# All 31 convolution taps of channel tile 7 on TensorE for both token chunks, as two token phases by 64 channels; and chunk A's first two output tiles side by side

## The chip, the cores and the metric

The kernel runs on one core of a Trainium2 chip. The metric is the device time of one execution in microseconds (us). The engines are named as the profile names them: PE is TensorE (PEld its weight load), DVE is VectorE, ACT is ScalarE, POOL is GpSimd, and SP is the queue that issues most of the loads. Line numbers such as L128 are those of the kernel before; two of its helper lines record nearly everything, L128 every instruction of DVE, ACT and POOL, and L151 every matmul, so groups are told apart by the names of their tiles.

## The reference

A decoder trunk of two layers on 1024 tokens of 1024 channels. The first layer mixes tokens with a causal Conformer convolution, the second with a multi-scale pooling mixer; each is followed by a SwiGLU feed-forward of width 2816. The change touches only the convolution:

```python
def conformer_conv(h, w1, b1, w_dw, b_dw, ln_g, ln_b, w2, b2):
    u = h @ w1 + b1
    a, g = jnp.split(u, 2, axis=-1)
    u = a * jax.nn.sigmoid(g)
    u = lax.conv_general_dilated(          # depthwise, causal, CONV_WIDTH = 31 taps
        u, w_dw[:, None, :], window_strides=(1,), padding=[(CONV_WIDTH - 1, 0)], ...) + b_dw
    u = jax.nn.silu(layer_norm(u, ln_g, ln_b))     # over the 1024 channels
    return u @ w2 + b2

def reference(...):
    for i in range(DEPTH):                 # DEPTH = 2
        ...                                # adaLN: shift, scale and gate columns from c
        h = modulate(rms_norm(x, norm_mix_g[i]), sh_m, sc_m)
        y = conformer_conv(h, ...) if i % 2 == 0 else multiscale_pool(h, ...)
        x = x + (1.0 + g_m)[:, None, :] * y
        h = modulate(rms_norm(x, norm_ffn_g[i]), sh_f, sc_f)
        x = x + (1.0 + g_f)[:, None, :] * swiglu_ffn(h, ...)
    return rms_norm(x, final_g)
```

## The kernel before

**Layout.** Channels lie on the 128 partitions, tokens on the free axis. The 1024 channels are 8 tiles (0 to 7), the 1024 tokens two chunks of 512: A (the first) and B. Matmuls run in a 32-bit format that rounds its operands, so each value is split into a high and a low part, and `products()` issues three matmuls for each product: high by high, high by low, low by high. A weight of 128x1024 arrives in a `raw` buffer (ring of three), ScalarE casts it to its high part (`w<-raw`), VectorE subtracts to get the low one (`w<-raw,w`), and the pair stays in a ring of five (`W_BUFS`) until its products are over. Some loads are issued on GpSimd's queue, most on SP's.

**The convolution module.** For each tile, `conv_in` multiplies h by w1 into two PSUM banks, `a` and `g`, 24 matmuls each. `conv_glu` takes ScalarE's sigmoid of g into `t`, and VectorE multiplies (`u<-a,vecs,t`). Then the 31 taps follow. Most are done by `Taps` tasks: on VectorE an accumulation in one of two extra PSUM banks (`ca<-u,vecs,ca`, one instruction for each tap; the first is `ca<-u,vecs` alone), or on ScalarE a product `pr` that GpSimd adds to a partial sum `pa`; at the end VectorE adds `pa` to `ca` and applies the last tap (`u<-u,vecs,ca`). Two tiles have taps on TensorE, by matmuls with diagonal matrices (`tap<-us,w`, us being the split u): 15 of tile 6's for chunk A, and all 31 of tile 7's for chunk A (`PE_TAPS = {6: 15, 7: CW}`, `pe_taps`). The diagonals come as six weights of eight blocks (`wdg`). Chunk B's tiles 6 and 7 are done by `Taps` like the others. The last 30 tokens of chunk A's u are kept in `uhalo` for chunk B.

**The layer norm** (`layer_norm_silu`) adds the eight convolved tiles on VectorE (`acc`; the seventh sum ends it), multiplies by a matrix of ones on PE (`mean<-acc,ones`), centres, squares, sums, takes the root (`var`, `rstd` on PE), and applies SiLU into the split pairs `v`. `conv_out` then multiplies by w2, one bank `y` for each output tile, and updates x.

**The order.** PE runs in the order in which the program is written, and that is the order of a list of units: chunk A's w1 tiles, the last of chunk A together with the same tiles of chunk B, most of chunk B's w1 tiles, the TensorE taps, the rest of chunk B's w1 tiles, w2 of chunk A, chunk B's last w1 tile, and the first feed-forward's head for chunk A (products `p` by w_gate and w_up, `dn` by w_down), in the course of which chunk B's taps and layer norm go on beside it; then w2 of chunk B. Between products, `pace()` lets the tasks of the other engines take steps as long as the planner's estimated clocks of these engines lie less than 4 us ahead of PE's. A task that needs PE yields a name of the table `DELAY`, and its next PE instruction is written that many estimated us later. VectorE, ScalarE, GpSimd and SP run their own queues in order, and an instruction waits only for its data and for a free buffer. The six ordinary PSUM banks serve all of `a`, `g`, `tap`, `mean`, `y` in turn.

The adaLN columns that the feed-forward needs first are handled amid the taps: `columns_done` sends sums `t` through PE (`adac<-quarters,t`), and VectorE adds a bias (`mod<-adac,vecs`).

Of the kernel before, what the change touches and what calls it, by code (L numbers as in the profile page):

```python
# [53 lines left out]
DIAGS = 8  # L54
LOAD = {"load": 4.0, "both": 9.5, "slow": 6.0, "next": 4.0, "dots": 4.0}
# [16 lines left out]
DELAY = {"stats": 2.75, "spread": 3.0, "soon": 0.5, "settled": 3.0, "later": 5.0, "root": 3.4}  # L72
# [4 lines left out]
for _name, _w in (  # L77
    ("ada_b", DEPTH * 6 * KT), ("norm_mix_g", DEPTH * KT), ("norm_ffn_g", DEPTH * KT),
    ("conv_b1", 2 * KT), ("conv_bdw", KT), ("conv_ln_g", KT), ("conv_ln_b", KT), ("conv_b2", KT),
    ("c", KT), ("pool_ls", KT), ("final_g", KT), ("conv_wdw", CW * KT),  # L80
):
    _COLS[_name] = _n
    _n += _w
# [18 lines left out]
def tap_groups(p):  # L102

    n = PE_TAPS[p]

    todo = list(range(CW - 1, -1, -1) if n == CW else range(CW - 3, CW - 3 - 2 * n, -2))
# [27 lines left out]
def trunk(ctx, tc, xT, c, vec, ada, adan, w1f, w1, wdg, w2, wgu, wdn, wds, wpl, out):  # L134
# [597 lines left out]
    def conv_u(ch, p):  # L732
        u = st["u", ch.i, p] = wslot(ch, "u", p)
        if ch.i == 0:
# [5 lines left out]
    def conv_glu(ch, p, ba, bg, own=False):  # L740
# [50 lines left out]

    def split_u(p):
# [6 lines left out]
    def pe_taps(p):  # L799
# [4 lines left out]
        for i, js in enumerate(groups):  # L804
            def emit(take, i=i, js=js):
# [3 lines left out]
                for q, j in enumerate(js):  # L809
                    full = PE_TAPS[p] == CW  # L810
                    o = (CW - 1 - j) // 2 * 2 if full else CW - 3 - j
                    c = j + o if full else 0
                    products(b[:, o:], wt, q, [v[:, c : c + A.n - o] for v in st["us", p]], j == groups[0][0], j == groups[-1][-1])
                    if q % 4 == 3:
                        pace()
                if i == len(groups) - 1:
                    if full:
                        S_.activation(st["u", 0, p][:, HALO:], b, AF.Identity, bias=V("conv_bdw", p))
                        st["taps", 0][p] = True
                    else:  # L820
                        T["taps", 0, p].other = b
# [86 lines left out]
    def layer_norm_silu(ch):  # L908
# [17 lines left out]
        yield "soon" if ch.i else "stats"  # L926
# [1330 lines left out]
```

## Time and profile before

| what | value |
|---|---|
| median of three runs | 1677.97 us (1677.6, 1677.97, 1678.09) |
| the profiled execution, its time | 1675.66 us |
| its span in the trace | 1673.9 us |
| PE busy | 1651.8 us, 7550 matmuls |
| DVE busy | 1310.0 us, 1867 instructions |
| ACT busy | 804.1 us, 1090 instructions |
| POOL busy | 487.4 us, 567 instructions |
| w1, taps and layer norm of chunk A | up to about 300 us |
| first feed-forward's head, with chunk B's taps and layer norm beside it | about 300 to 460 us |

Of the views below, the page gives busy time by engine and the chain of work that ended last. A row of the windows begins with the window's bounds in us and its length; then come the busy us and the instructions in brackets for PE, PEld, DVE, ACT and POOL; then the granted clock of PE, the DMA engines' share and the GB/s moved. A row of the waits reads: engine, tile and line, what released it, the total us, the count, the longest. A row of the timeline reads: start, length, engine, line, operation, out<-in, shape, and behind an x how many instructions of that kind are put together; in square brackets the wait before it and what ended it. A row of groups ends with the busy us and the mean ns of one, and behind the last bar the idle time before them and what ended most of it.

Convolution's place in the time: the adaLN columns of PE come at 181 us, the last TensorE tap at about 200 us, chunk A's mean at 205 us, chunk B's at 417 us.

### The profile page before, as it was taken

The numbers are of one execution on the slowest core, as the hardware profiler recorded it, in microseconds if no ns is written. First come the engines' busy times: TensorE is split into PE (matmuls) and PEld (weight loads), VectorE is DVE, ScalarE is ACT, GpSimd is POOL, SyncE is SP. The second block draws the span as 40 slices with busy tenths as digits, with TensorE's granted clock in tenths as the row PEclk, the third lists the DMA queues.
The fourth block names the chain that finished last, engine by engine and source line by source line (L and its number), as shares of the span: only waits on it lengthen the run. The fifth ranks groups of instructions, "written<-read, shape, count | busy, mean of one in ns | idle before, by whom it ended". The sixth has DMA issues, their size and how long they took to land.

```text
span 1673.9 us, 21194 instructions
## 1 busy us (share of the span) xinstructions
PE 1651.8 (99%) x7550; PEld 1351.2 (81%) x7550; DVE 1310.0 (78%) x1867; ACT 804.1 (48%) x1090; POOL 487.4 (29%) x567
## 2 busy tenths in 40 slices
PE   7999999999999999999999999999999999999997
PEld 5777878787888888888888888888888888888887
DVE  8889899799759888888678957848777766658657
ACT  3669696867546332332234436637322222244354
POOL 3587777796002111221100502101111111000013
PEclk9999999999999999999999999999999999999999
DMA  8958997828776888886965959866777776686664
GB/s 301 295 176 228 225 236 205 226 78 241 229 234 168 278 264 287 282 272 206 400 231 164 285 155 283 247 211 199 189 225 222 220 227 183 207 273 207 192 170 126
DMA packets 117180, 378.60 MB, mean 226 GB/s; under 512 B 12369, under 2 KB 14545, under 8 KB 117074
## 3 DMA queue, kind: packets, MB, share of 16 engines
q1 hardware_dynamic: 79664, 245.63, 41.6%
q0 software_dynamic: 36832, 131.09, 32.5%
q8 instruction: 59, 0.97, 0.2%
q10 hardware_dynamic: 578, 0.53, 0.1%
q14 instruction: 47, 0.39, 0.1%
HBM read 310.61 MB, written 62.39 MB: 223 GB/s over the span
## 4 chain that ended last, share of the span: by engine, by line
PE 88%; POOL 3%; DVE 2%; DMA 2%; issue 2%; ACT 2%; DVEq 0%; SPq 0%; POOLq 0%; ACTq 0%
PE a L151 24%; PE dn L151 23%; PE e L151 14%; PE p L151 10%; PE y L151 6%; POOL pa L128 3%; PE first L151 3%; PE g L151 2%; PE tap L151 2%; DMA adaw<-in_adan_dram 1%; DMA s<-in_wds_dram 1%; PE ada L151 1%; ACT w L128 1%; DMA w<-in_wgu_dram 1%; PE var L151 1%
## 5 line engine op out<-in xcount | busy, mean ns | idle before, releaser
L128 ACT CAST w<-raw 128x1024 fp32r<-128x1024 f32 (+1 forms) x247 | 254.6, 1033 | 305.5 <-PE dn L151 56.9
L128 DVE TENSOR_TENSOR w<-raw,w 128x1024 fp32r<-128x1024 f32 (+1 forms) x173 | 209.3, 1214 | 62.2 <-ACT w L128 61.9
L151 PE MATMUL a<-n,w 128*128 128x512 f32 x1056 | 246.8, 389 | 0.2
L151 PE MATMUL p<-h,w 128*128 128x512 f32 x1056 | 243.7, 390 | 1.2 <-DMA w<-in_wgu_dram 1.0
L128 POOL TENSOR_TENSOR pa<-pa,pr 128x512 f32<-128x512 f32 x159 | 225.3, 1500 | 29.0 <-ACT pr L128 23.7
L151 PEld LDWEIGHTS p<-h,w 128*128 128x128 f32 x1056 | 197.3, 188 | 43.7 <-DMA w<-in_wgu_dram 1.4
L151 PEld LDWEIGHTS a<-n,w 128*128 128x128 f32 x1056 | 198.0, 188 | 42.2 <-DVE r L128 1.1
L151 PE MATMUL dn<-hi,w 128*128 128x512 f32 (+1 forms) x768 | 226.2, 377 | 0.4 <-DVE w L128 0.4
L151 PE MATMUL dn<-g,w 128*128 128x512 f32 x864 | 199.1, 390 | 0.2 <-DVE x L128 0.2
L151 PEld LDWEIGHTS dn<-g,w 128*128 128x128 f32 x864 | 161.7, 188 | 34.7 <-DVE x L128 0.6
L128 DVE SCALAR_TENSOR_TENSOR ca<-u,vecs,ca 128x512 f32<-128x512 f32 x246 | 170.6, 747 | 0.5
L151 PEld LDWEIGHTS dn<-hi,w 128*128 128x128 f32 x768 | 141.2, 188 | 27.0 <-DVE w L128 0.9
L151 PE MATMUL dn<-lo,w 128*128 128x512 f32 (+1 forms) x384 | 144.3, 376 | 0.0
L151 PE MATMUL a<-t,w 128*128 128x512 f32 x528 | 123.3, 389 | 0.0
L151 PE MATMUL e<-t,w 128*128 128x512 f32 x528 | 123.3, 389 | 0.0
L151 PE MATMUL e<-b,w 128*128 128x512 f32 x528 | 123.3, 389 | 0.0
L128 ACT ACTIVATE pr<-u,vecs 128x512 f32<-128x512 f32 x159 | 108.4, 717 | 25.0 <-POOL pa L128 19.7
L151 PEld LDWEIGHTS a<-t,w 128*128 128x128 f32 x528 | 99.1, 188 | 20.7
L151 PEld LDWEIGHTS e<-t,w 128*128 128x128 f32 x528 | 99.1, 188 | 20.6
L151 PEld LDWEIGHTS e<-b,w 128*128 128x128 f32 x528 | 99.1, 188 | 20.6
L1191 POOL DMA_DIRECT2D raw<-in_wgu_dram x41 | 36.5, 889 | 271.5 <-DVE r L128 104.2
L128 ACT CAST hi<-op 128x1024 fp32r<-128x1024 f32 (+1 forms) x52 | 48.5, 935 | 87.1 <-PE dn L151 77.2
(191 smaller groups left out, 2449.4 us busy)
## 6 DMA issues: line engine op xcount, KB each, us to landing
raw<-in_wgu_dram SPq DMA_DIRECT2D x132, 512.0 KB, 4.7
raw<-in_wds_dram SPq DMA_DIRECT2D x48, 512.0 KB, 6.0
adaw<-in_ada_dram POOLq DMA_DIRECT2D x48, 512.0 KB, 6.8
kinds<-k POOLq DMA_DIRECT2D x42, 512.0 KB, 7.7
raw<-in_wgu_dram POOLq DMA_DIRECT2D x41, 512.0 KB, 7.3
raw<-in_w_dram SPq DMA_DIRECT2D x36, 512.0 KB, 6.6
op<-kinds SPq DMA_DIRECT2D x36, 512.0 KB, 4.8
adaw<-in_adan_dram SPq DMA_DIRECT2D x32, 512.0 KB, 5.5
```

Source lines behind the costliest of these rows:

```text
L128: self.last = self.order(getattr(self.eng, name)(out, *args, **kw))
L151: last_mm[0] = nc.tensor.matmul(out, lhsT, rhs, start=start, stop=stop, skip_group_check=more).ins.name
L1191: d = order(nc.gpsimd.dma_start(w[i], wgu[l, fp, src], accum_op=ADD))
```

## The change

Tile 7 leaves the `Taps` tasks altogether. Its u is no longer kept as 128 channels by 512 tokens: `halves` stacks the even tokens of 64 channels on partitions 0 to 63 and the odd tokens of the same 64 channels on partitions 64 to 127, once for each half g of the channels, for both chunks in one buffer (15 zero columns in front, then 256 token pairs of A, then 256 of B). A matrix of 128x128 then holds up to four taps (from either phase to either phase) for each of 64 channels, and 16 such blocks with shifts of whole pairs cover the 31 taps. One product is 512 columns wide and serves both chunks at once: 2 groups of 16 blocks of 3 matmuls, 96, in place of 31 times 3, 93, of 512 down to 482 columns for chunk A alone. The number of weights stays at six. Each group's bank is written back to u's ordinary layout by four ScalarE instructions of 64x256.

With it the mean of chunk A gets a delay of its own in the planner's table (4.6 in place of 2.75), and `conv_out` of chunk A puts its first two output tiles side by side as that of chunk B did.

By instructions, PE has 3 matmuls more; DVE has 17 `ca<-u,vecs,ca` fewer, eight instructions of 64x256 more, and some single ones fewer, 13 fewer in sum; ACT has 4 fewer in sum (11 `pr` fewer); POOL has 14 fewer in sum (11 `pa` fewer).

```diff
@@ constants, and one row of the table of planning delays
+HALF = P // 2          # 64 channels
+NM = (CW + 1) // 2     # 16 blocks
+LEAD = NM - 1          # 15 token pairs of history
-DELAY = {"stats": 2.75, "spread": 3.0, ...
+DELAY = {"mean": 4.6, "stats": 2.75, "spread": 3.0, ...

@@ conv_u: tile 7's u needs no halo in front
         u = st["u", ch.i, p] = wslot(ch, "u", p)
+        if PE_TAPS.get(p) == CW:
+            return u

@@ conv_glu: tile 7
-        if ch.i == 0 and PE_TAPS.get(p) == CW:
-            V_.scalar_tensor_tensor(ba, ba, V("conv_b1", p), sg, op0=ADD, op1=MUL)
-            pair = wpair(B, "us", F32R)
-            hi, lo = st["us", p] = [pair[:, i, : ch.width] for i in range(2)]
-            for part in (hi, lo):
-                G_.memset(part[:, HALO - 2 : HALO].bitcast(F32), 0.0)
-            S_.copy(hi[:, HALO:], ba)
-            V_.tensor_tensor(lo[:, HALO:], ba, hi[:, HALO:].bitcast(F32), op=SUB)
-            S_.copy(uhalo[:, p, :], ba[:, ch.n - HALO :])
+        if PE_TAPS.get(p) == CW:
+            halves(ch, p, ba, sg)
             return

@@ new: u by token phase (f) and channel half (g)
+    def halves(ch, p, ba, sg):
+        n = ch.n // 2
+        t = temp(ch.n).rearrange("p (g n) -> p g n", g=2)
+        for g in range(2):
+            at = slice(HALF * g, HALF * g + HALF)
+            for f in range(2):
+                V_.scalar_tensor_tensor(t[HALF * f : HALF * f + HALF, g], ba[at].rearrange("p (n f) -> p f n", f=2)[:, f], V("conv_b1", p)[at],
+                                        sg[at].rearrange("p (n f) -> p f n", f=2)[:, f], op0=ADD, op1=MUL)
+        if ch.i == 0:
+            st["us", p] = [wpair(B, "us", F32R) for _ in range(2)]
+            for part in st["us", p]:
+                G_.memset(part[:, :, :LEAD].bitcast(F32), 0.0)
+        hi, lo = (part[:, :, LEAD + ch.i * n : LEAD + ch.i * n + n] for part in st["us", p])
+        S_.copy(hi, t)
+        V_.tensor_tensor(lo, t, hi.bitcast(F32), op=SUB)

@@ new: the taps of tile 7, both chunks in one product of 512 columns
+    def pe_halves(p):
+        blocks = [(g, m) for g in range(2) for m in range(NM)]
...
+                    if m == 0:
+                        st["tap", p] = bank("tap")
+                    b = st["tap", p]
+                    products(b, wt, q, [part[:, g, m : m + 512] for part in st["us", p]], m == 0, m == NM - 1)
+                    if q % 4 == 3:
+                        pace()
+                    if m == NM - 1:
+                        for ch in chunks:
+                            n = ch.n // 2
+                            d = st["u", ch.i, p][HALF * g : HALF * g + HALF, HALO:].rearrange("p (n f) -> p f n", f=2)
+                            for f in range(2):
+                                at = slice(HALF * f, HALF * f + HALF)
+                                S_.activation(d[:, f], b[at, n * ch.i : n * ch.i + n], AF.Identity, bias=V("bdw_halves", g)[at])
+                            if g:
+                                st["taps", ch.i][p] = True
...

@@ pe_taps: the case of all 31 taps
                 for q, j in enumerate(js):
-                    full = PE_TAPS[p] == CW
-                    o = (CW - 1 - j) // 2 * 2 if full else CW - 3 - j
-                    c = j + o if full else 0
-                    products(b[:, o:], wt, q, [v[:, c : c + A.n - o] for v in st["us", p]], j == groups[0][0], j == groups[-1][-1])
+                    o = CW - 3 - j
+                    products(b[:, o:], wt, q, [v[:, : A.n - o] for v in st["us", p]], j == groups[0][0], j == groups[-1][-1])
...
-                    if full:
-                        S_.activation(st["u", 0, p][:, HALO:], b, AF.Identity, bias=V("conv_bdw", p))
-                        st["taps", 0][p] = True
-                    else:
-                        T["taps", 0, p].other = b
+                    T["taps", 0, p].other = b

@@ layer_norm_silu: the planner's delay between acc and the mean
-        yield "soon" if ch.i else "stats"
+        yield "soon" if ch.i else "mean"

@@ conv_out: the output tiles that share a unit
-        for ds in [(0, 1) if ch.i else (0,), *(() if ch.i else ((1,),)), *((d,) for d in range(2, KT))]:
+        for ds in [(0, 1), *((d,) for d in range(2, KT))]:

@@ trunk
     for p in PE_TAPS:
-        for u in pe_taps(p):
+        for u in pe_halves(p) if PE_TAPS[p] == CW else pe_taps(p):
             unit(*u)
...
-    taps(B, *some, *rest[: len(rest) - HOLD - HOLD_LN])
+    taps(B, *[p for p in some if PE_TAPS.get(p, 0) < CW], *rest[: len(rest) - HOLD - HOLD_LN])

@@ host: the weights of the blocks (dense 128 x 128 in place of diagonals)
+    dense = np.zeros((len(whole), 2, NM, 2, HALF, 2, HALF), np.float32)
+    for i, p in enumerate(whole):
+        for m in range(NM):
+            for f in range(2):
+                for o in range(2):
+                    j = 2 * (m - LEAD) + CW - 1 + f - o
+                    if 0 <= j < CW:
+                        dense[i, :, m, f, range(HALF), o, range(HALF)] = taps[j, p].reshape(2, HALF).T
+    dense = dense.reshape(-1, DIAGS, P, P).transpose(0, 2, 1, 3)
```

Since the planner writes the order, three places show what it makes of the change. First VectorE, from the adaLN columns on (`mod`), ahead of chunk A's mean; ca_1559 and ca_1591 before, ca_1566 and ca_1622 after, are the tap banks of chunk A's last two `Taps` tiles, acc_1453 and acc_1459 the sum of the tiles. Before:

```order
L128 TENSOR_TENSOR mod<-adac_1792,vecs 128x8
L128 SCALAR_TENSOR_TENSOR ca_1559<-u_721,vecs,ca_1559 128x512
L128 SCALAR_TENSOR_TENSOR ca_1591<-u_721,vecs,ca_1591 128x512
L128 SCALAR_TENSOR_TENSOR ca_1559<-u_721,vecs,ca_1559 128x512
L128 SCALAR_TENSOR_TENSOR ca_1591<-u_721,vecs,ca_1591 128x512 x3
L128 TENSOR_TENSOR ca_1559<-pa_1529,ca_1559 128x512
L128 SCALAR_TENSOR_TENSOR ca_1591<-u_721,vecs,ca_1591 128x512
L128 SCALAR_TENSOR_TENSOR u_721<-u_721,vecs,ca_1559 128x512
L128 SCALAR_TENSOR_TENSOR ca_1591<-u_721,vecs,ca_1591 128x512
L128 TENSOR_TENSOR acc_1453<-acc_1453,u_721 128x512
```

And now, the start and (from the end of the first tile on) the corresponding rows:

```order
L130 TENSOR_TENSOR mod<-adac_1796,vecs 128x8
L130 SCALAR_TENSOR_TENSOR ca_1622<-u_721,vecs,ca_1622 128x512
L130 SCALAR_TENSOR_TENSOR ca_1566<-u_721,vecs,ca_1566 128x512
...
L130 SCALAR_TENSOR_TENSOR ca_1622<-u_721,vecs,ca_1622 128x512
L130 TENSOR_TENSOR ca_1566<-pa_1556,ca_1566 128x512
L130 SCALAR_TENSOR_TENSOR ca_1622<-u_721,vecs,ca_1622 128x512
L130 SCALAR_TENSOR_TENSOR u_721<-u_721,vecs,ca_1566 128x512
L130 SCALAR_TENSOR_TENSOR ca_1622<-u_721,vecs,ca_1622 128x512
L130 TENSOR_TENSOR acc_1459<-acc_1459,u_721 128x512
```

Between `mod` and the partial sum's addition (`ca<-pa,ca`) stood 6 taps and now stand 17; from `mod` to the last sum of acc, in all, there were 33 instructions, 21 of them such taps, and there are 41, 29 of them taps.

Second PE, at the end of the TensorE taps, where chunk A's mean stands. Before:

```order
L151 MATMUL tap_1779<-us_1229,w_1735 128x484 x6
L151 MATMUL tap_1779<-us_1229,w_1735 128x482 x3
L151 MATMUL a_1975<-h_801,w_1769 128x512 x3
...
L151 MATMUL a_1975<-h_808,w_1769 128x512 x3
L151 MATMUL mean_2010<-acc_1962,ones 128x512
L151 MATMUL g_1976<-h_801,w_1829 128x512 x3
```

And now:

```order
L153 MATMUL tap_1889<-us_1233,w_1742 128x512
L153 MATMUL tap_1889<-us_1232,w_1742 128x512
L153 MATMUL a_1996<-h_801,w_1776 128x512 x3
...
L153 MATMUL a_1996<-h_808,w_1776 128x512 x3
L153 MATMUL mean_2031<-acc_1983,ones 128x512
L153 MATMUL g_1997<-h_801,w_1834 128x512 x3
```

The mean stands at the same place, behind the 24 matmuls of the next w1 tile's `a`; what moved is its operand's chain on VectorE.

Third PE in the feed-forward's head, where chunk B's mean stands. Before:

```order
L151 MATMUL p_3852<-h_2808,w_3749 128x512 x3
L151 MATMUL dn_3974<-g_3744,w_3796 128x512 x3
L151 MATMUL dn_3975<-g_3744,w_3796 128x512 x3
L151 MATMUL dn_3976<-g_3744,w_3796 128x512 x3
L151 MATMUL dn_3977<-g_3744,w_3796 128x512 x3
L151 MATMUL mean_3990<-acc_3961,ones 128x512
L151 MATMUL dn_3974<-g_3843,w_3848 128x512 x3
```

And now:

```order
L153 MATMUL p_3763<-h_2838,w_3592 128x512 x3
L153 MATMUL p_3763<-h_2839,w_3592 128x512 x3
L153 MATMUL p_3763<-h_2840,w_3592 128x512 x3
L153 MATMUL mean_3791<-acc_3748,ones 128x512
L153 MATMUL p_3667<-h_2841,w_3609 128x512 x3
```

It moved 108 matmuls ahead, out of the `dn` products into the `p` products before them; the `var` and `rstd` products behind it follow in their turn.

More of the change, by code (lines that the diff above doesn't have):

```diff
@@ L71 @@
 LATER = 300
-DELAY = {"stats": 2.75, "spread": 3.0, "soon": 0.5, "settled": 3.0, "later": 5.0, "root": 3.4}
+DELAY = {"mean": 4.6, "stats": 2.75, "spread": 3.0, "soon": 0.5, "settled": 3.0, "later": 5.0, "root": 3.4}
 DELAY_BEHIND = {"stats": 8, "spread": 4, "soon": 0.5, "settled": 3.0, "later": 8}
@@ L79 @@
     ("conv_b1", 2 * KT), ("conv_bdw", KT), ("conv_ln_g", KT), ("conv_ln_b", KT), ("conv_b2", KT),
-    ("c", KT), ("pool_ls", KT), ("final_g", KT), ("conv_wdw", CW * KT),
+    ("c", KT), ("pool_ls", KT), ("final_g", KT), ("conv_wdw", CW * KT), ("bdw_halves", 2),
 ):
@@ L104, in tap_groups @@
     n = PE_TAPS[p]
-    todo = list(range(CW - 1, -1, -1) if n == CW else range(CW - 3, CW - 3 - 2 * n, -2))
+    todo = list(range(CW - 3, CW - 3 - 2 * n, -2))
     return [todo[i : i + DIAGS] for i in range(0, len(todo), DIAGS)]
@@ L790, in conv_in, with emit_of, emit @@
         unit(emit, *[w1[p, i] for p in tiles for i in range(2)])
+    def halves(ch, p, ba, sg):
[15 more added lines that the diff above has]
+        blocks = [(g, m) for g in range(2) for m in range(NM)]
+        first = sum(len(tap_groups(q)) for q in PE_TAPS if q < p)
+        def emit_of(these):
+            def emit(take):
+                wt = take()
+                for q, (g, m) in enumerate(these):
+                    if m == 0:
[13 more added lines that the diff above has]
+                                st["taps", ch.i][p] = True
+            return emit
+        return [(emit_of(blocks[i : i + DIAGS]), wdg[first + i // DIAGS]) for i in range(0, len(blocks), DIAGS)]
     def split_u(p):
@@ L2207 @@
         ada_b, norm_mix_g, norm_ffn_g, conv_b1, conv_bdw, conv_ln_g, conv_ln_b, conv_b2, c, pool_ls, final_g, conv_wdw)])
+    whole = [p for p in PE_TAPS if PE_TAPS[p] == CW]
+    vec = np.concatenate([vec, np.tile(np.asarray(conv_bdw).reshape(KT, 2, HALF)[whole].reshape(-1, HALF), (1, 2))])
     def tiles(w, f):
@@ L2219 @@
     taps = np.asarray(conv_wdw)[0].reshape(CW, KT, P)
-    groups = [(p, js) for p in sorted(PE_TAPS) for js in tap_groups(p)]
+    groups = [(p, js) for p in sorted(PE_TAPS) if PE_TAPS[p] < CW for js in tap_groups(p)]
     diag = np.zeros((len(groups), P, DIAGS, P), np.float32)
@@ L2224 @@
             diag[i, range(P), q, range(P)] = taps[j, p]
+    dense = np.zeros((len(whole), 2, NM, 2, HALF, 2, HALF), np.float32)
[7 more added lines that the diff above has]
+    dense = dense.reshape(-1, DIAGS, P, P).transpose(0, 2, 1, 3)
+    diag = np.concatenate([diag, dense])
     down = np.asarray(ffn_w_down).reshape(DEPTH, NP, 2, P, 2, D // 2)
@@ L2238 @@
         "w1": A(np.stack([t1[:KT], t1[KT:]], axis=1)),
-        "wdg": A(diag.reshape(len(groups), P, -1)),
+        "wdg": A(diag.reshape(len(diag), P, -1)),
         "w2": A(tiles(np.asarray(conv_w2)[0], KT)),
```

## The prediction

> **What bounds the kernel now.** I read the page first, then the windows, then PE's waits, then the timelines around each place that the change touches. The page:
>
> ```profile
> span 1673.9 us, 21194 instructions
> PE 1651.8 (99%) x7550; PEld 1351.2 (81%) x7550; DVE 1310.0 (78%) x1867; ACT 804.1 (48%) x1090; POOL 487.4 (29%) x567
> PE 88%; POOL 3%; DVE 2%; DMA 2%; issue 2%; ACT 2%; DVEq 0%; SPq 0%; POOLq 0%; ACTq 0%
> ```
>
> TensorE is busy for 99% of the span and carries 88% of the chain. A window in the feed-forward shows its pace, and PE's waits between 60 and 460 us, where all of the changed work lies, are these four:
>
> ```profile
> 700.00:800.00 100.00, 100.00 (x443) 82.81 (x442) 81.20 (x111) 28.85 (x34) 19.48 (x34) 1.00 0.79 249
> ...
> PE p L151 <- DMA w<-in_wgu_dram: 1.0, 1, 1.0
> PE ada L151 <- DMA adaw<-in_adan_dram: 0.3, 1, 0.3
> PE dn L151 <- DVE x L128: 0.2, 1, 0.2
> PE p L151 <- ACT r L128: 0.2, 1, 0.2
> ```
>
> 443 products in 100 us are 0.226 us each. All four waits together are 1.7 us. So work that leaves VectorE, ScalarE and GpSimd here cannot make the kernel faster by more than 1.7 us: PE does not wait for it. What can cost is work added to PE, or a product that now stands ahead of its operand.
>
> **The change part by part.** *PE's own work.* Tile 7 took 31 taps of three products for chunk A, 512 down to 482 columns wide. It now takes 32 blocks of three products, all 512 wide, for both chunks. By the order, 12 products stand ahead of the adaLN columns (adac) in both kernels; then 81 stood before chunk A's next w1 product, and now 84.
>
> ```profile
> 181.16 0.51 PE L151 MATMUL adac<-quarters,t 128*128 128x4 f32 x4
> 181.52 18.61 PE L151 MATMUL tap<-us,w 128*128 128x508 f32 x81
> ...
> 199.97 5.62 PE L151 MATMUL a<-h,w 128*128 128x512 f32 x24
> 205.43 1.02 PE L151 MATMUL mean<-acc,ones 128*128 128x512 f32 x2
> ```
>
> The 81 took 199.97 - 181.52 = 18.45 us. The 24 behind them took 205.43 - 199.97 = 5.46 us, 0.2275 each, and 84 such take 19.11 us: +0.66 us, all of it on PE's path. The first group of 12 changes by less than 0.05 us.
>
> *Chunk A's mean.* This is where I expect the loss. The order puts the mean product behind 24 products of the next w1 tile, as before, so PE is there at 205.43 + 0.66 = 206.09 us. Its operand acc is the sum of the eight convolved tiles, made on VectorE. That chain before:
>
> ```profile
> 169.38 0.67 ACT L128 ACTIVATE t<-g,vecs 128x512 f32<-128x512 f32 x1
> ...
> 170.08 0.75 DVE L128 SCALAR_TENSOR_TENSOR u<-a,vecs,t 128x512 f32<-128x512 f32 x1
> 170.75 9.30 DVE L128 SCALAR_TENSOR_TENSOR ca<-u,vecs,ca 128x512 f32<-128x512 f32 x14
> 181.70 0.17 DVE L128 TENSOR_TENSOR mod<-adac,vecs 128x8 f32<-128x8 f32 x1 [1.65 <-PE adac L151]
> 181.78 4.30 DVE L128 SCALAR_TENSOR_TENSOR ca<-u,vecs,ca 128x512 f32<-128x512 f32 x6
> ...
> 203.35 1.50 DVE L128 TENSOR_TENSOR acc<-acc,u 128x512 f32<-128x512 f32 x2
> ```
>
> VectorE runs in order and waits 1.65 us for adac, which PE reaches at 181.16 us. So everything behind the mod instruction starts at 181.78 us, however early VectorE was. From there to acc it was busy all but about 0.5 us:
>
> ```profile
> L128 DVE SCALAR_TENSOR_TENSOR ca<-u,vecs,ca 128x512 f32<-128x512 f32 x21 | 14.8, 750 | 0.1
> L128 DVE TENSOR_TENSOR ca<-pa,ca 128x512 f32<-128x512 f32 x3 | 2.1, 693 | 0.3 <-POOL pa L128 0.2
> ```
>
> acc ended at 203.35 + 1.50 = 204.85 us, 0.58 us ahead of the mean. The order shows what the change does behind mod: 29 tap instructions (ca) where there were 21, the 12 others as before. The planner has moved eight chunk-A taps from ahead of mod, where VectorE waits anyway, to behind it. Ahead of mod the anchor is unchanged: the GLU of chunk B's tile 1 and 14 taps stand in both kernels, and they ended 1.65 us early. A tap's pace is (9.30 - 0.75) / 13 = 0.658 us, so eight add 5.26 us; the 0.2 us wait for GpSimd's partial sum goes, since that will be long done. acc is then ready at 204.85 + 5.26 - 0.2 = 209.9 us. How soon a mean follows its acc is seen at chunk B, where PE came just in time:
>
> ```profile
> 415.83 0.69 DVE L128 TENSOR_TENSOR acc<-acc,u 128x512 f32<-128x512 f32 x1
> ...
> 416.66 1.10 PE L151 MATMUL mean<-acc,ones 128*128 128x512 f32 x2
> ```
>
> That is 0.15 us after 416.52. So chunk A's mean starts at 210.06 us, PE stands for 4.0 us, and everything behind it on PE (the other half of the tile, the layer norm, w2, the feed-forward) is 210.06 - 205.43 = **4.6 us later**, the 0.66 us included. The bounds are 1.2 us, if acc is early (96 x 512 columns for 46,176 before, at 0.0004425 us each), and 5.5 us, if GpSimd's sums are late as well. I take 4.6 since each row of the sum is there.
>
> *The halves.* Building them is eight 64x256 instructions on VectorE (four for each chunk) for two of 128x512, and one more 128x512 subtraction. The trace has no 64x256 instruction; the nearest rows are:
>
> ```profile
> L128 DVE SCALAR_TENSOR_TENSOR x<-dn,gains,x 128x256 f32<-128x256 f32 x8 | 3.8, 479 | 1.2 <-PE dn L151 1.0
> L128 ACT ACTIVATE t<-x 128x256 f32<-128x256 f32 x8 | 3.3, 418 | 11.0 <-DVE x L128 10.9
> ```
>
> With the same free size I take 0.48 us; the bounds are 0.15 (the 128x4 rows) and 0.75 us. That is 3.8 - 1.5 + 0.6 = +2.9 us of VectorE, all ahead of mod. It is covered: nine taps fewer stand ahead of mod (5.9 us), so the 1.65 us wait there stays whole. If that cover were gone, the mean would be later still by the overrun. Writing back is eight ScalarE instructions at about 0.42 us, in place of one of 0.69. Chunk A's last two end some 1.0 us after the last tap, at 202 us, and the sum that reads them stands last, at 209 us: hidden. Chunk B's 31 taps of tile 7 leave VectorE (which loses 17 tap instructions in all) and ScalarE with GpSimd (11 and 11 fewer); by the waits above that is worth nothing to PE, and no more do the two small copies and the clearing for the halo that go with them.
>
> [...]
>
> *Behind the mean.* The layer norm's chain gains on PE:
>
> ```profile
> 206.58 1.06 ACT L128 ACTIVATE w<-raw 128x1024 fp32r<-128x1024 f32 x1
> 207.54 0.57 ACT L128 COPY ny<-mean 128x512 f32<-128x512 f32 x1
> ```
>
> ScalarE copied the mean 2.1 us after it began, because two weight casts stood ahead; those will be over when PE is 4.6 us late, so the chain restarts about 1 us sooner against PE. Up to the w2 products every wait was zero before, and stays so. Putting the first two output tiles side by side lets PE need the last normed tile after 42 products and not 21, 4.8 us later; it did not wait there, so that is worth 0 (0 to 0.2). The second weight is needed 5.3 us earlier, but its load stands four weights ahead in the queue: 0.
>
> *Chunk B's mean* now stands 108 products (24.5 us) earlier on PE: at 416.66 + 4.6 - 24.5 = 396.8 us. VectorE before:
>
> ```profile
> 378.00 1.40 DVE L128 SCALAR_TENSOR_TENSOR x<-dn,gains,x 128x512 f32<-128x512 f32 x2
> 379.32 11.93 DVE L128 SCALAR_TENSOR_TENSOR ca<-u,vecs,ca 128x512 f32<-128x512 f32 x18
> ```
>
> By the order, between chunk A's mean and the last of these x updates stand two taps and a sum more and one initial tap less (+1.2 us), so it ends at 379.4 + 4.6 + 1.2 = 385.2 us. Behind it are 12 taps (7.9 us) and five closing instructions (3.2 us): acc at 396.3 us, ready at 396.5. I take 0, with 0 to 1.5 us as bounds, as the spare is 0.3 us. Layer norm, casts and weight loads behind it run beside 144 products instead of 54 up to w2: 0 (0 to 2 us, if the raw buffer of the fourth down weight, which a VectorE subtraction behind the root frees, is filled late).
>
> *The weight from GpSimd's queue.*
>
> ```profile
> 376.92 0.91 POOL L506 DMA_DIRECT2D w<-in_wgu_dram  x1
> ...
> 386.81 1.43 PE L151 MATMUL p<-h,w 128*128 128x512 f32 x5 [1.01 <-DMA w<-in_wgu_dram]
> ```
>
> The accumulating load came 1.0 us late, 9.8 us after its issue. Eleven partial sums stand ahead of it where ten and an initial one stood, so GpSimd gains nothing by itself; PE comes later. I take -0.4 us (0 to -1.0).
>
> **The sum**: +4.6 - 0.4 = +4.2 us. The profiled execution took 1675.66 us with its 1.76 us around the span; the median of the runs shown is 1677.97 us, 2.3 us above it. The same sum on the median gives **1682.2 us**.
>
> **The rivals.** *PE's clock drops in the stall* (chance 0.12). After the idle start PE ran at half pace for some us:
>
> ```profile
> 21.00:23.30 2.30, 2.30 (x6) 1.73 (x6) 2.30 (x5) 0.00 (x0) 0.00 (x0) 1.00 0.14 32
> ...
> 26.00:28.00 2.00, 2.00 (x11) 1.65 (x10) 2.00 (x5) 0.00 (x0) 2.00 (x1) 1.00 0.77 311
> ```
>
> Six products in 2.3 us against eleven in 2.0. No wait of PE from 60 to 460 us is longer than 1.0 us, so nothing here shows whether 4.0 us suffice to fall back. If they do, the products behind the mean run at half pace for some 4 us and lose about 2: 1684.2 us. [...]
>
> *The stall is given back* (0.15), which ends not slower by what can be told: the GpSimd load above is the one place where PE lost a whole us. If it lands before PE's later arrival, 1.0 us returns, and with an acc 0.3 us earlier the time is 1677.97 + 4.6 - 1.3 = 1681.3 us. It decides at 1.0 us of gain of the issue on PE. For it: PE is 4.6 us late. Against it: the ring of weights is freed by PE, so the issue moves with PE.
>
> *acc is not late at all* (0.08): 1677.97 + 1.2 = 1679.2 us. It needs VectorE to pass mod 4 us sooner; the order of both engines speaks against it.
>
> *A second stall at chunk B* (0.09): its mean or the fourth down weight costs 1.5 us or more, 1683.7 to 1686 us. For it: 0.3 us of spare. Against it: GpSimd and VectorE have fewer taps to end there.
>
> **How the numbers follow.** The likeliest case (0.53) is the stall alone, 1681.0 to 1683.5 us; 0.03 is left for a gain that I don't see. A change of 0.2%, 3.4 us, is about what a measurement of this kernel tells from none, so slower begins at 1681.3 us. Of the likeliest case 0.05 lies below that; with the clock (0.12), the second stall (0.09) and 0.01 of the giving back, slower has 0.70; same has 0.05 + 0.14 + 0.08 = 0.27; faster 0.03. The range 1678.6 to 1685.2 us leaves out the second stall's far end, and the lower part of the early acc.
>
> **What would show it.** PE's waits have a new first row, mean behind DVE acc, near 4.0 us; mod on VectorE still waits for adac; PE's next product after the mean comes 4.6 us later than before; chunk B's mean waits under 1 us; from 450 us on every stage keeps its length. A mean without a wait refutes the main step; a granted clock below 1 behind 210 us makes the clock's case.

## The result: 1700.88 us, slower by 1.3%

The changed kernel took 1700.88 us (median of 1697.08, 1701.64, 1701.48 and 1700.29); the kernel before, beside it, 1678.03 us. The ratio is 1.013, with a 95% interval of 1.0112 to 1.0148. The forecast was 1682.2 us, and its range ended at 1685.2 us: the sign was right and the size was not, by 18.7 us. The profiled execution took 1697.08 us, the shortest of the four, at a granted clock of 0.995 over the span; the other three had 0.993.

The page of the changed kernel, profiled execution:

```profile
span 1695.3 us, 21158 instructions
PE 1657.6 (98%) x7553; PEld 1355.5 (80%) x7553; DVE 1308.1 (77%) x1854; ACT 802.1 (47%) x1086; POOL 471.9 (28%) x553
PE 77%; DVE 7%; ACT 4%; POOL 3%; issue 2%; DMA 2%; DVEq 0%; POOLq 0%; ACTq 0%
```

PE's share of the chain fell from 88% to 77%, and what came in its place is work of VectorE and ScalarE. PE's waits between 60 and 480 us, which stood at 1.7 us in all (60 to 460 us) before, now read:

```profile
PE y L153 <- ACT t L130: 4.6, 1, 4.6
PE p L153 <- ACT r L130: 4.5, 2, 4.2
PE mean L153 <- DVE acc L130: 3.6, 2, 3.4
PE a L153 <- ACT t L130: 2.2, 2, 1.1
PE ada L153 <- DMA adaw<-in_adan_dram: 1.2, 1, 1.2
PE p L153 <- DMA w<-in_wgu_dram: 1.1, 1, 1.1
```

The prediction has the third row, and the last one, which stood there before at 1.0 us. To place the 21.4 us between the two spans, here is PE's timeline at the same points of the program, before:

```profile
167.31 1.88 PE L151 MATMUL tap<-us,w 128*128 128x512 f32 x7
...
238.91 1.45 PE L151 MATMUL y<-v,w 128*128 128x512 f32 x5
...
449.92 1.30 PE L151 MATMUL y<-v,w 128*128 128x512 f32 x5
...
532.88 2.43 PE L151 MATMUL a<-n,w 128*128 128x512 f32 x10
```

and after:

```profile
170.66 1.65 PE L153 MATMUL tap<-us,w 128*128 128x512 f32 x6
...
184.85 19.80 PE L153 MATMUL tap<-us,w 128*128 128x512 f32 x84
204.49 5.64 PE L153 MATMUL a<-h,w 128*128 128x512 f32 x24
213.53 0.67 PE L153 MATMUL mean<-acc,ones 128*128 128x512 f32 x1 [3.40 <-DVE acc L130]
...
247.11 0.98 PE L153 MATMUL y<-v,w 128*128 128x512 f32 x3
252.67 3.91 PE L153 MATMUL y<-v,w 128*128 128x512 f32 x9 [4.58 <-ACT t L130]
...
465.31 5.49 PE L153 MATMUL p<-h,w 128*128 128x512 f32 x12 [4.20 <-ACT r L130]
470.60 1.74 PE L153 MATMUL y<-v,w 128*128 128x512 f32 x5
...
554.03 2.20 PE L153 MATMUL a<-n,w 128*128 128x512 f32 x9
```

| stretch of PE's program | before, us | after, us | more |
|---|---|---|---|
| to the first tap | 167.31 | 170.66 | 3.4 |
| first tap to chunk A's mean (205.43 before) | 38.12 | 42.87 | 4.8 |
| mean to the first w2 product of chunk A | 33.48 | 33.58 | 0.1 |
| from there to the first w2 product of chunk B | 211.01 | 223.49 | 12.5 |
| from there to the first pooling product (a<-n) | 82.96 | 83.43 | 0.5 |

Behind that nothing changes. Of the first 3.4 us, two waits of 1.1 us for a sigmoid (the row a behind ACT t) and 0.9 us more for an adaLN load are the larger part. Two of the timeline's rows show a second loss beside the wait: nine y matmuls took 3.91 us, and twelve p matmuls took 470.60 - 465.31 = 5.29 us, 0.44 us each where 0.23 is PE's pace. The clock had fallen to half:

```profile
253.01:256.40 3.39, 3.39 (x10) 2.62 (x9) 3.03 (x5) 3.21 (x6) 3.08 (x3) 0.50 1.01 237
...
465.91:471.45 5.54, 5.54 (x14) 4.28 (x13) 1.90 (x3) 1.49 (x3) 0.00 (x0) 0.50 0.85 271
```

The column of the granted clock reads 0.50 in both windows. So each of these two stalls cost its wait and a stretch at half pace behind it: 4.6 + 1.7 us for y, 4.2 + 2.6 for p (and 0.4 more in the y products behind it, which is most of the 0.5 in the table's last row). That is 13.1 us, of which 0.6 was regained elsewhere in the stretch, at places that these rows do not show. These are the 12.5 us that the prediction did not have.

### The profile page after: what moved, and what is told of

It reads as the page before. It is cut to its first block, busy times and chain, and to the rows that moved or that the text cites. A ratio compares the mean times of both kernels' runs of the same rounds, so it can differ in the third digit from the quotient of the medians.

```text
span 1695.3 us, 21158 instructions
## 1 busy us (share of the span) xinstructions
PE 1657.6 (98%) x7553; PEld 1355.5 (80%) x7553; DVE 1308.1 (77%) x1854; ACT 802.1 (47%) x1086; POOL 471.9 (28%) x553
## 4 chain that ended last, share of the span: by engine, by line
PE 77%; DVE 7%; ACT 4%; POOL 3%; issue 2%; DMA 2%; DVEq 0%; POOLq 0%; ACTq 0%
PE dn L153 23%; PE a L153 22%; PE e L153 14%; PE p L153 10%; PE y L153 7%; DVE ca L130 3%; POOL pa L130 3%; ACT w L130 2%; DMA raw<-in_w_dram 1%; ACT x L130 1%; DVE u L130 1%; DMA raw<-in_wgu_dram 1%; ACT pr L130 1%; PE g L153 1%; DVE h L130 0%
## 5 line engine op out<-in xcount | busy, mean ns | idle before, releaser
L130 POOL TENSOR_TENSOR pa<-pa,pr 128x512 f32<-128x512 f32 x148 | 211.8, 1510 | 30.3 <-ACT pr L130 27.7
L130 DVE SCALAR_TENSOR_TENSOR ca<-u,vecs,ca 128x512 f32<-128x512 f32 x229 | 159.0, 746 | 0.7
L130 ACT ACTIVATE pr<-u,vecs 128x512 f32<-128x512 f32 x148 | 101.3, 717 | 35.3 <-POOL pa L130 25.8
L153 PE MATMUL y<-v,w 128*128 128x512 f32 x384 | 90.8, 397 | 4.6 <-ACT t L130 4.6
```

The costliest lines, as they stand in the source:

```text
L130: self.last = self.order(getattr(self.eng, name)(out, *args, **kw))
L153: last_mm[0] = nc.tensor.matmul(out, lhsT, rhs, start=start, stop=stop, skip_group_check=more).ins.name
```

## The experiments

Each time is the median of four or five executions, run beside the kernel before; "loss" is that median less the one of the kernel before beside it, and the changed kernel's own loss is 22.9 us. The diffs show only the lines that matter, with ... for what is left out of a line; angle brackets describe an argument.

### The output tiles: which operand was late?

Three stalls were new: y, p, and the small ones ahead of the taps. The first run undoes the side-by-side tiles alone:

```diff
-        for ds in [(0, 1), *((d,) for d in range(2, KT))]:
+        for ds in [(0, 1) if ch.i else (0,), *(() if ch.i else ((1,),)), *((d,) for d in range(2, KT))]:
```

> The changed kernel, but chunk A's first two output tiles one after the other again, as before the change. Bank theory: the second of the two side-by-side banks is still the g bank of chunk B's last w1 tile and comes free only with ScalarE's sigmoid, which stands behind the layer norm's SiLUs. Alone, the first output tile needs one bank, so PE's wait of 4.6 us after the third y matmul goes, and with it the nine matmuls at half pace (1.8 us) behind it: 6.4 us less, about 1694.5 us. Rival, the norm's values: y waits for the normed tiles v, which come no earlier; then PE still waits 3 us or more in this y tile, and the time stays above 1698 us.

Measured 1693.3 us, a loss of 16.1 us (ratio 1.0097, 1.0081 to 1.0112). PE's waits there:

```profile
PE p L153 <- ACT r L130: 4.8, 1, 4.8
...
PE y L153 <- DVE u L130: 0.6, 1, 0.6
```

The wait of y fell from 4.6 to 0.6 us, and no product behind it ran at half pace. So the normed tiles were not late; a bank was. The order on ScalarE in the changed kernel shows which:

```profile
250.64 1.28 ACT L130 ACT_TABLE_LOAD   x1
251.93 0.69 ACT L130 ACTIVATE t<-g,vecs 128x512 f32<-128x512 f32 x1
```

This sigmoid empties the g bank of chunk B's last w1 tile. It is held behind the layer norm's SiLUs and the table load of 1.28 us in the row above it, and PE goes on at 252.67 us, 0.05 us after it ends. The counterpart puts the side-by-side tiles, and nothing else, into the kernel before:

```diff
-        for ds in [(0, 1) if ch.i else (0,), *(() if ch.i else ((1,),)), *((d,) for d in range(2, KT))]:
+        for ds in [(0, 1), *((d,) for d in range(2, KT))]:
```

> The kernel before with one line changed: chunk A's first two output tiles side by side, nothing else. Bank theory: the sigmoid that frees the g bank ended at 243.9 us, the second output tile would need its bank at 239.6 us: PE waits 4.2 us, and the matmuls behind run at half pace for a while (1 to 2.5 us): about 1683 us. Rival: the wait belongs to the late layer norm of the changed kernel; in the kernel before the two tiles side by side cost nothing, 1677.5 us.

Measured 1687.45 us against 1676.3, a loss of 11.2 us (ratio 1.0068, 1.0056 to 1.0081), some 4 us more than expected. ScalarE and PE there:

```profile
245.92 0.69 ACT L128 ACTIVATE t<-g,vecs 128x512 f32<-128x512 f32 x1
...
246.66 0.50 PE L151 MATMUL y<-v,w 128*128 128x512 f32 x1 [4.04 <-ACT t L128]
```

The wait came as worked out, 4.04 us, again ended by that sigmoid, and seven products behind it ran at half pace. The rest is waits that came with the planner's new order, 2.3 us at chunk B's mean and 1.5 us for a copied bank, and in the profiled execution (1690.95 us, the longest of the five) two more stretches at half pace, behind an adaLN load and at that mean. One line costs more alone than its share in the changed kernel.

### The wait ahead of the last p products

The chain of it, in the changed kernel: a sum of two loaded quarters of the next unit's weights stands on VectorE ahead of a weight's low part (453.38 us); the low part frees a raw buffer; SP then issues w2's next raw loads; ScalarE's cast waits for one, and the copy r, which frees PE's bank, stands behind the cast. VectorE, then SP, then ScalarE:

```profile
453.38 1.23 DVE L130 TENSOR_TENSOR s<-raw,raw 128x1024 f32<-128x1024 f32 x1 [5.07 <-DMA raw<-in_wgu_dram]
454.52 1.22 DVE L130 TENSOR_TENSOR w<-raw,w 128x1024 fp32r<-128x1024 f32 x1
...
455.77 0.85 SPq L498 DMA_DIRECT2D raw<-in_w_dram  x2
...
463.73 1.04 ACT L130 CAST w<-raw 128x1024 fp32r<-128x1024 f32 x1 [7.43 <-DMA raw<-in_w_dram]
464.68 0.58 ACT L130 COPY r<-p 128x512 f32<-128x512 f32 x1
```

Two things can be at fault, the sum's place on VectorE or the loads that it waits for. First the sum alone was moved:

```diff
+            if fp == 0 and l == 0:
+                tc.add_manual_dep(summed.ins, <low part of the third directly split w2 weight>, ...)
```

> The changed kernel with one instruction moved: VectorE's sum of two quarters of the feed-forward's joint weights (s<-raw,raw, with the next sum that uses it) is held behind the low part of the third directly split w2 weight of chunk B, where it stood before the change. Order theory: the sum waits 5.1 us for its load and blocks the low part behind it, which frees the raw buffer of the next w2 weight; that load lands late, ScalarE's cast waits for it, and the copy that frees PE's bank stands behind the cast. Without it the wait of 4.2 us ahead of the last p products goes, and the 13 matmuls at half pace (2.7 us): 7 us less, about 1694 us. Rival, the transfer: the w2 loads are late because the DMA engines are full of the joint quarters and of x written out; then the raw load still lands late, PE still waits 2 us or more there, and the time stays above 1698 us.

Measured 1697.91 us, a loss of 20.7 (ratio 1.0117, 1.0103 to 1.0131). PE still waited 2.4 us at this place and ran at half pace behind it: neither reading is right alone, and the expected 7 us are missed. So the loads were held as well (the sum follows them):

```diff
-        nc.sync.dma_start(raw, wgu[l, fp, i])
+        d = nc.sync.dma_start(raw, wgu[l, fp, i])
+        if l == 0 and fp == 0:
+            tc.add_manual_dep(d.ins, <load of the third directly split w2 weight>, ...)
```

> The changed kernel with SP's four loads of the joint weights' quarters (feed-forward) held behind the load of the third directly split w2 weight, about where they stood before the change; no other load moves. Transfer theory: these 2 MB, with the two accumulating loads behind them, were pulled ahead of w2's loads because chunk B's layer norm frees their buffers 24 us earlier, and the raw w2 loads that ScalarE's cast waits for need 8 to 12 us to land instead of 5 to 7. Held back, the wait of 4.2 us ahead of the last p products goes, with the half-paced matmuls behind it: 6 to 7 us less than the changed kernel, about 1694 us. Rival, the order on VectorE alone: the sum that waited for the quarters was the cause; holding only the sum took 3 us, and holding the loads as well takes no more, about 1698 us, PE still waiting over 2 us there.

Measured 1693.95 us, a loss of 17.7 (ratio 1.0102, 1.0086 to 1.0117). PE's waits:

```profile
PE y L153 <- DMA w<-in_w_dram: 1.2, 1, 1.2
PE p L153 <- ACT r L130: 0.3, 1, 0.3
```

The wait for r is 0.3 us and no product runs at half pace there; a new wait of 1.2 us for a w2 weight appears behind it. The DMA issues say why the loads mattered: 512 KB of w2, issue to landing, in the changed kernel (436 to 464 us) first, in this one (430 to 458 us) second:

```profile
raw<-in_w_dram SPq DMA_DIRECT2D x5, 512.0 KB, 8.5
```

```profile
raw<-in_w_dram SPq DMA_DIRECT2D x5, 512.0 KB, 4.0
```

In the median the same five loads took 4.0 us and not 8.5 once the quarters stood behind them. What had pulled the quarters ahead may be chunk B's early layer norm, which frees their buffers: the next run moves chunk B's mean back by the planner's delay and holds nothing.

```diff
-DELAY = {"mean": 4.6, ...
+DELAY = {"mean": 4.6, "mean_b": 25.0, ...
-        yield "soon" if ch.i else "mean"
+        yield "mean_b" if ch.i else "mean"
```

> The changed kernel with the planner's delay of chunk B's mean at 25 instead of 0.5, so that this mean stands on PE about where it stood before the change (141 matmuls ahead of w2's products; before 150, changed 258). If chunk B's early layer norm is the root of the quarters' early loads, the quarters' loads stand again behind the first w2 loads, PE's wait of 4.2 us ahead of the last p products and its half-paced matmuls go, and the time falls by 6 to 7 us to about 1694 us, as when the loads alone were held. Rival: the early loads come from the changed feed-forward units and not from the norm; then the wait stays above 3 us and the time near 1700 us.

Measured 1695.43 us, a loss of 17.7 (ratio 1.0109, 1.0095 to 1.0123). PE waits 0.5 us for r in all, and SP issues the quarters again behind three of w2's loads (from 460.4 us, the three from 456.0 us). So the place of that norm is the root. Why the planner put it 108 products earlier is read from its order, not tested: the change had taken work from VectorE, ScalarE and GpSimd ahead of it. The run has a loss of its own, a wait of 2.7 us (1.1 in the changed kernel) for a weight from GpSimd's queue, with half pace behind it.

### VectorE and GpSimd: the halves' low part

In the changed kernel three VectorE instructions with both operands in SBUF took some five times as long as their like elsewhere. First the subtraction as it was in the kernel before, with one operand (`a`) in PSUM, beside four of GpSimd's sums (128.43 to 133.93 us):

```profile
129.46 0.68 DVE L128 TENSOR_TENSOR us<-a,us 128x512 fp32r<-128x512 f32 x1
```

Then the changed kernel, VectorE first and GpSimd beside the last of the three:

```profile
130.42 3.49 DVE L130 TENSOR_TENSOR us<-t,us 128x512 fp32r<-128x512 f32 x1
...
137.79 3.23 DVE L130 TENSOR_TENSOR acc<-u 128x512 f32<-128x512 f32 x1
...
161.22 3.91 DVE L130 TENSOR_TENSOR us<-t,us 128x512 fp32r<-128x512 f32 x1 [0.93 <-ACT us L130]
...
161.16 3.42 POOL L130 TENSOR_TENSOR pa<-pa,pr 128x512 f32<-128x512 f32 x2
```

Each ends some 0.6 us after GpSimd's run of sums does. ScalarE's products share a ring of buffers with the halves and wait for this subtraction; behind them eleven instructions on x (twelve in a row before, from 128.91 us) now run late, ahead of a sigmoid that PE waits for:

```profile
133.95 0.72 ACT L130 ACTIVATE pr<-u,vecs 128x512 f32<-128x512 f32 x1 [3.96 <-DVE us L130]
...
137.09 6.84 ACT L130 ACTIVATE x<-x,gate_b 128x512 f32<-128x512 f32 x11
143.83 0.67 ACT L130 ACTIVATE t<-g,vecs 128x512 f32<-128x512 f32 x1
```

So the halves were put into PSUM, into the g bank that the sigmoid has read:

```diff
-        t = temp(ch.n).rearrange("p (g n) -> p g n", g=2)
+        t = bg.rearrange("p (g n) -> p g n", g=2)
```

> The changed kernel with the stacked halves of u written into the g bank (PSUM) instead of an SBUF buffer, so that the subtraction for the low part has one operand in PSUM. Contention theory: with both operands in SBUF that subtraction lasts 3.5 and 3.9 us because VectorE is held while GpSimd adds its partial sums; with one in PSUM it takes 0.7 us as before the change. ScalarE's products pr, which wait for its buffer, come 3 us sooner, the sigmoids are in time, and PE's two waits of 1.1 us for a bank at 143 and 157 us go: 2.2 us less, about 1698.5 us; chunk A's mean still waits 3 us or more. Rival, the shape: the subtraction is slow because its output is cut into two pieces of 256; then it stays at 3 us or more and the time at 1700.9 us.

Measured 1697.15 us, a loss of 19.9 (ratio 1.0117, 1.0104 to 1.0131).

```profile
160.82 0.69 DVE L130 TENSOR_TENSOR us<-g,us 128x512 fp32r<-128x512 f32 x1 [0.66 <-ACT us L130]
```

The subtraction takes 0.69 us with its two pieces of 256, beside three of GpSimd's sums (160.29 to 164.21 us): the shape is not the cause, the operands are. The first sum `acc<-u`, whose operands are still both in SBUF, took 4.07 us in this run, again beside three of GpSimd's. The two waits for a sigmoid went, and one of 2.8 us for the bank came in their place. Against the expectation the mean's wait fell to 0.3 us; the planner had left 37 instructions behind `mod` instead of 41.

So beside GpSimd's sums the subtraction took 3.91 us with both operands in SBUF, and 0.69 with one in PSUM; by what means it is so slow in the first case no run shows. The one at 161.22 us began 0.06 us behind the first of GpSimd's two sums and ended 0.55 us behind the second.

The three edits together (the sum held, not yet the loads):

> The changed kernel with all three edits: first output tiles one after the other, the quarters' sum held back, the halves in PSUM. If the three losses are separate they add: 6.4 + 7 + 2.2 = 15.6 us less, about 1685 us, and what is left against the kernel before is the wait of chunk A's mean, near 4 us, the 0.7 us of PE's own work, and the earlier wait for an adaLN load (0.9 us). Rival: the waits stand in for each other, so that taking one away uncovers the next; then the sum is under 10 us and the time above 1691 us.

Measured 1688.81 us, a loss of 11.6 (ratio 1.007, 1.0057 to 1.0082): 11.3 us back where 15.6 were expected, between the two theories. The shortfall has names: the wait for r was still 3.4 us, and the bank's 2.8, each with a stretch at half pace behind it.

### What adds up

With the first two output tiles one after the other and the quarters' loads held:

> The changed kernel with chunk A's first two output tiles one after the other and the quarters' loads held back. If the bank wait and the late w2 loads are separate, 7.6 us (measured for the first) and 6.5 us add: about 1686.5 us. What is left against the kernel before, 9 us, is the mean's wait with PE's own work (4.8), two waits of 1.1 us for a sigmoid, a load waited for at 90 us, and the half pace behind them. Rival: the second wait comes back because all of PE's schedule moves with the first; then above 1690 us.

Measured 1690.42 us, a loss of 14.1 (ratio 1.0082, 1.0068 to 1.0096): 8.8 us back, where the two alone gave 6.8 and 5.2. This missed the expected 1686.5 us. In its profile, of the longest of the four executions (1692.62 us), PE waits 3.0 us for adaLN loads (1.2 in the changed kernel's) and runs at half pace behind one of them, and again behind the mean's stall of 3.0 us, where the changed kernel's profile has none. Why those loads come late stays open.

Then the halves' low part on GpSimd, which also tests what makes chunk A's mean late ("port theory" is a name for the contention theory of above; no run shows a port):

```diff
         S_.copy(hi, t)
-        V_.tensor_tensor(lo, t, hi.bitcast(F32), op=SUB)
+        G_.tensor_tensor(lo, t, hi.bitcast(F32), op=SUB)
```

> The changed kernel with the first two output tiles one after the other, the quarters' loads held back, and the low part of the halves subtracted on GpSimd instead of VectorE (the planner then gives tile 6's low part to VectorE). By the port theory VectorE loses no 7 us to two subtractions, ScalarE's products are not held up, and PE's two waits of 1.1 us at 143 and 157 us go. By the order theory of chunk A's mean, 39 instructions stand between mod and the last sum (33 before, 41 in the changed kernel), at 0.68 us each, and PE waits 2.3 us at the mean; by the port theory alone, which puts the late sum down to the lost time, it waits under 1 us. Both give about 1687 us; a mean's wait above 1.5 us decides for the order.

Measured 1686.7 us, a loss of 8.9 (ratio 1.0062, 1.0048 to 1.0075). VectorE, and PE's waits:

```profile
182.49 0.17 DVE L130 TENSOR_TENSOR mod<-adac,vecs 128x8 f32<-128x8 f32 x1 [1.02 <-PE adac L153]
...
207.94 1.50 DVE L130 TENSOR_TENSOR acc<-acc,u 128x512 f32<-128x512 f32 x2
```

```profile
PE mean L153 <- DVE acc L130: 3.2, 2, 2.0
```

VectorE waits for adac again, acc comes 27.0 us after `mod`, and the mean waits 2.0 us (the other 1.2 are chunk B's) where the order theory had 2.3 and the port theory less than 1. The sigmoid waits are gone. Other runs bear the order out: from `mod` to the end of acc it is 23.2 us with 33 instructions (the kernel before), 25.2 with 37 (the halves in PSUM), 27.0 with 39 and 28.0 with 41. With the halves in PSUM instead:

> The changed kernel with the first two output tiles one after the other, the quarters' loads held back, and the halves in the g bank (PSUM). 37 instructions stand between mod and the last sum; the mean waits 0.5 us as it did with the halves in PSUM alone. The bank wait of 2.8 us near 157 us stays. Against 1690.4 us without the halves in PSUM: 2.2 us for the sigmoid waits and 2.8 for the mean, less 2.8 for the bank, about 1688 us. If it is above 1690 us the halves cost as much in PSUM as in SBUF.

Measured 1684.98 us, a loss of 7.2 (ratio 1.0044, 1.0032 to 1.0057), better than the 1688 expected; the bank wait stayed (2.9 us).

### The place of chunk A's mean

```diff
-DELAY = {"mean": 4.6, ...
+DELAY = {"mean": 7.5, ...
```

> The changed kernel with the planner's delay of chunk A's mean at 7.5 instead of 4.6: the mean stands 12 matmuls (2.7 us) later on PE, behind half of the g matmuls of that w1 tile. Chain theory: the sum on VectorE and the layer norm behind it set the time, so the wait at the mean falls from 3.6 to about 0.9 us and PE waits 2.7 us longer at the output tiles, where the sigmoid is no earlier: 1700.9 us, within 1.5 us. Rival, the place: the mean stands too early on PE, and later it costs nothing elsewhere: 2.7 us less or more, 1698 us.

Measured 1697.92 us, a loss of 21.6 (ratio 1.0123, 1.0109 to 1.0137). The median is the rival's; against the kernel before beside it the gain is 1.2 us, which is the chain theory's. PE waits 3.9 us for y instead of 4.6, and not 2.7 longer, so the chain theory's mechanism failed; but chunk B's mean now waits 4.9 us. With this much moving at once the run decides little. On top of the repaired version it does:

> The version with the first two output tiles one after the other, the quarters' loads held back and the halves' low part on GpSimd (1686.7 us), with chunk A's mean 12 matmuls later on PE besides. It tells apart two readings of the 3 us that the later mean gave alone. Slack reading: the layer norm's chain does not start late enough to delay the output tiles, so the 2.1 us wait at the mean and the half-paced matmuls behind it (1.2 us) go and nothing comes for them: 1683.5 us. Chain reading: the sum on VectorE sets when the output tiles can run, PE waits some 2 us there instead, and only the half pace goes: 1685.5 us or more. No reading puts it below the kernel before (1677.5): PE's own 0.7 us, the load waited for at 90 us and the late w2 load behind the layer norm of chunk B (1.5 us) stay.

Measured 1683.36 us, a loss of 5.8 (ratio 1.0036, 1.0022 to 1.0049). No wait at chunk A's mean is left and none has come at the output tiles:

```profile
PE ada L153 <- DMA adaw<-in_adan_dram: 2.1, 2, 1.2
...
PE mean L153 <- DVE acc L130: 1.2, 1, 1.2
PE y L153 <- DMA w<-in_w_dram: 1.0, 1, 1.0
```

(the mean in that row is chunk B's). The slack reading is right: the norm behind the mean has room, and the wait at the mean was a matter of where PE's order put it. No stretch at half pace is left between 60 and 480 us either. This is the best version found, 17 us ahead of the changed kernel, and still slower than the kernel before; beyond these rows, what makes up the 5.8 us stays open.

## Why the prediction was right and wrong

**What bounds the kernel: right.** The work taken from the other engines gained nothing. It cost instead, through the queues that it re-ordered.

**Chunk A's mean: right.** `mod` at 185.41 us, acc done 28.0 us later (28.1 forecast from 41 instructions), PE's stall 3.4 us where 4.0 were forecast:

```profile
185.41 0.16 DVE L130 TENSOR_TENSOR mod<-adac,vecs 128x8 f32<-128x8 f32 x1
...
211.89 1.50 DVE L130 TENSOR_TENSOR acc<-acc,u 128x512 f32<-128x512 f32 x2
```

The stretch to the mean grew by 4.8 us; 4.6 was the forecast. Two of its terms were off all the same. *PE's own work* was sized at 0.66 us: 84 matmuls were priced like the w1 products at 0.2275 us, but the taps took (204.49 - 184.85) / 84 = 0.234 each, and the term is 1.2 us. The prediction's own rows had this pace, since the 81 narrower taps before took 18.45 us for 40,134 columns, 0.235 us for 512. (Its bound for the columns has slips: tile 7 had 46,266 of them, not 46,176, which is 0.04 us; and its 0.0004425 us for a column stands in no row, but lies between the prediction's two paces, 0.226 / 512 = 0.000441 and 0.2275 / 512 = 0.000444.) The mean came no later for it, since acc sets the mean; PE only came later to wait for it, 3.4 us in place of 4.0. And `mod` did not wait for adac, which was there at 184.99 us; VectorE came 0.4 us later than that. That the halves cost VectorE just its cover and 0.4 us more, so that the forecast of this stretch still held, is luck.

**The halves: the step that failed is "+2.9 us of VectorE, all ahead of mod. It is covered".** The eight 64x256 instructions took 0.48 us each, as taken from the 128x256 row. The "one more 128x512 subtraction" was put at 0.6 us without a row for it. With both operands in SBUF, and GpSimd's sums beside them, chunk A's and chunk B's took 3.5 and 3.9 us. The claim that "the 1.65 us wait there stays whole" failed with it: the cover was used up and `mod` came 0.4 us late. And ScalarE waited for that buffer (6.7 us in two waits), which the prediction never followed, so that PE lost 2.2 us to two late sigmoids.

**The output tiles: the step that failed is "that is worth 0 (0 to 0.2)".** It asked when the last normed tile and the second weight were needed, and not where the second bank came from. 4.6 us of wait and 1.7 at half pace followed; taking the tiles apart gave 6.8 us of loss back.

**Chunk B's mean: the step that failed is "0 (0 to 2 us ...)".** The mean itself was in time. But the step looked for one down weight behind it, and did not ask what else the early norm sets free: four loads of 512 KB that SP had queued behind the fifth of w2's loads now went ahead of the third. 4.2 us of wait and 3.0 at half pace followed; holding those loads gave 5.2 us back.

**The clock: mechanism right, place and chance wrong.** The rival put a fall of the clock behind the mean's stall, at a chance of 0.12, which was the author's estimate, and a price of 2 us. Behind that stall the profiled execution shows none. But of the seven profiles, of the changed kernel and its variants, with a stall of 2.0 us or more at chunk A's mean, four show one there, so the chance was too small. Its price was about right: 1.7 us for the shorter of the stretches measured. Behind the two stalls that the prediction lacked, the clock cost some 4.7 us. Whether the example that it was taken from is one stays open: the slow products at 21 us stand in rows with a granted clock of 1.00, but the trace holds no record of the clock ahead of 23.30 us, and there their pace went from some 0.43 us each to 0.23. The other three executions of the changed kernel took 3 to 4.6 us longer, at a granted clock lower by 0.002 of the span; that fits two or three more stretches of 1.7 us, but no trace shows where they lay.

**Given back, acc not late, a second stall:** the first two did not happen. A second stall was real, but at neither of the two waits that the rival named; and its price, 1.5 us or more, left out the half-paced stretch behind it. The load from GpSimd's queue was late by 1.1 us as before, not 0.4 less.

## What to carry to other kernels

Where one engine is the bound, taking work from the others is not always free: it can move the instructions that wait only for a buffer. For each buffer and bank that comes free earlier, ask which load or product takes it and what that then stands in front of, and for each product moved forward ask which bank it writes to and what empties it, before asking for its operands. And price every stall of the bound engine with the stretch at half pace that may follow it, which cost 1.7 or 3.4 us here.

## What the runs showed of the hardware

PE's clock fell behind shorter stalls than the 4.0 us that the prediction asked about, and not behind each. Two windows of the run with the halves in PSUM alone, and one of the run with the low part on GpSimd, all at a granted 0.50:

```profile
93.85:97.24 3.39, 3.39 (x10) 2.62 (x8) 3.39 (x8) 2.21 (x4) 3.39 (x4) 0.50 1.05 332
...
401.49:404.47 2.98, 2.98 (x8) 2.31 (x7) 2.77 (x5) 0.06 (x1) 0.61 (x1) 0.50 1.06 276
```

```profile
211.13:213.69 2.56, 2.56 (x7) 1.98 (x6) 2.13 (x4) 1.78 (x4) 2.08 (x2) 0.50 1.00 245
```

The waits ahead of them were 1.0 us (adaLN load), 2.6 us and 2.0 us; the 3.4 us at the mean in the changed kernel was followed by none. These windows run from matmul to matmul. Read in steps of 0.05 us, the granted clock between 60 and 480 us of all these profiles is at half in 26 stretches, and each is 3.4 us long, or in four cases twice that; the changed kernel's own two begin at 253.04 us, for 3.4, and at 464.66 us, for 6.8. A stretch so costs a running PE 1.7 us, or 3.4. It begins between 2.3 us before PE resumes and 2.5 us after. All eleven waits of 3.7 us or more came with one; of the shorter ones some did. What sets the length of 3.4 us, and which of the shorter waits bring a stretch, no run shows.
